# Softmax times V: eight adjacent rows in each partition, one row block as the unit of work, and the transposed probabilities as the stationary operand

## The chip, the cores and the metric

The kernel runs on one core of a Trainium2 chip. The metric is the device time of the whole program in microseconds, as the median of several timed runs. A separate, profiled execution gives the trace from which all durations are read.

## What is computed

```python
def setup_inputs():
    batch, n_heads, seq, head_dim = 8, 12, 1024, 64
    # scores: randn (8, 12, 1024, 1024) float32; v: randn (8, 12, 1024, 64) float32

def reference(scores, v):
    scores_max = np.max(scores, axis=-1, keepdims=True)
    attn = np.exp(scores - scores_max)
    attn = attn / (np.sum(attn, axis=-1, keepdims=True) + 1e-8)
    return np.matmul(attn, v).astype(np.float32)
```

There are 8 x 12 = 96 independent heads. Each one reads a score matrix of 1024 x 1024 fp32 numbers (4 MB) and a V of 1024 x 64 (256 KB), and writes 1024 x 64 (256 KB). Both kernels take the exponential without the row maximum, convert it to fp16, append a column of ones to V, so that the product also gives the row sums, and divide by them at the end.

## The kernel before

One pass of the loop over n works on one head. SyncE issues all DMAs. The load at L64 puts the head's scores into `s_nat` so that partition p holds rows p, 128 + p, 256 + p and so on: eight runs of 4 KB in each partition. V (L69) and the output (L151) are laid out in the same way, in runs of 256 bytes. `s_nat`, `p_nat` and most other tiles have two buffers.

ScalarE takes the exponential of the whole head in one instruction (L83, 8192 columns, into the fp16 tile `p_nat`) and converts V into `vones` (L91); VectorE writes its column of ones (L90). TensorE then needs the probabilities with the key index in the partitions. For each of the eight column blocks `jb` it transposes eight 128 x 128 blocks (L112) into a PSUM tile `psumT`, and VectorE copies the 1024 columns to SBUF as `pt` (L118). Two blocks later come the products (L101): `vones` of that block, 128 x 65, is the stationary operand, `pt` moves past it in two halves of 512 columns, and two PSUM tiles `psO` gather the 65 x 1024 result over the eight blocks. In a product or transpose the stationary operand is loaded first, by a LDWEIGHTS of its own (PEld in the profile).

The result then lies with the output column in the partitions. VectorE copies it to `outT` (L76), TensorE transposes it back in eight fp32 pieces (`psX`, L135), and VectorE takes the reciprocal of each piece's row sums (L143) and scales it (L144). The store at L151 follows. In the source the last steps of head n stand in the pass of head n + 1 (`prev`).

A scheduling layer fixes the order of each engine's instructions when the program is built; on each engine they then run in that order. In the steady state SyncE has the store of head n, then V of head n + 2 and the scores of head n + 3, one after the other. An instruction at the front of SyncE's order that waits holds up all behind it.

Of the kernel before, what the change touches and what calls it, by code (L numbers as in the profile page):

```python
# [1 line left out]

# [5 lines left out]

FP32 = mybir.dt.float32
FP16 = mybir.dt.float16  # L10


@with_exitstack
def kernel(
    ctx: ExitStack,
    tc: tile.TileContext,
    scores: bass.AP,
    v: bass.AP,
    out: bass.AP,
):  # L20
    nc = tc.nc
    P = 128

    B, H, SQ, SK = scores.shape
    Bv, Hv, SKv, D = v.shape
    assert (B, H, SK) == (Bv, Hv, SKv)
    BH = B * H
    assert SQ % P == 0 and SK % P == 0
    NIB = SQ // P
    NJB = SK // P  # L30
    CH = min(512, SQ)
    NCH = SQ // CH
    M = D + 1
    assert M <= P
    MMLAG = min(2, NJB)

    sc_bh = scores.rearrange("b h i j -> (b h) i j")
    v_bh = v.rearrange("b h j d -> (b h) j d")
    out_bh = out.rearrange("b h i d -> (b h) i d")

    const_pool = ctx.enter_context(tc.tile_pool(name="const", bufs=1))
    s_pool = ctx.enter_context(tc.tile_pool(name="spool", bufs=2))
    p_pool = ctx.enter_context(tc.tile_pool(name="ppool", bufs=2))
    v_pool = ctx.enter_context(tc.tile_pool(name="vpool", bufs=2))
    pt_pool = ctx.enter_context(tc.tile_pool(name="ptpool", bufs=4))
    ot_pool = ctx.enter_context(tc.tile_pool(name="otpool", bufs=2))
    ob_pool = ctx.enter_context(tc.tile_pool(name="obpool", bufs=2))
    rc_pool = ctx.enter_context(tc.tile_pool(name="rcpool", bufs=2))
    psT_pool = ctx.enter_context(tc.tile_pool(name="psTp", bufs=4, space=bass.MemoryType.PSUM))
    psO_pool = ctx.enter_context(tc.tile_pool(name="psOp", bufs=2, space=bass.MemoryType.PSUM))  # L50
    psX_pool = ctx.enter_context(tc.tile_pool(name="psXp", bufs=2, space=bass.MemoryType.PSUM))

    ident32 = const_pool.tile([P, P], FP32, name="ident32")
    make_identity(nc, ident32)
    ident16 = const_pool.tile([P, P], FP16, name="ident16")
    nc.vector.tensor_copy(out=ident16[:], in_=ident32[:])  # L56

    prev = None

    for n in range(BH + 1):  # L60
        cur = None
        if n < BH:
            s_nat = s_pool.tile([P, NIB, SK], FP32, tag="s_nat")
            nc.sync.dma_start(  # L64
                out=s_nat[:],
                in_=sc_bh[n].rearrange("(ib p) j -> p ib j", p=P),
            )
            v_sb = v_pool.tile([P, NJB, D], FP32, tag="v_sb")
            nc.sync.dma_start(  # L69
                out=v_sb[:],  # L70
                in_=v_bh[n].rearrange("(jb p) d -> p jb d", p=P),
            )

        if prev is not None:
            for c in range(NCH):
                nc.vector.tensor_copy(  # L76
                    out=prev["outT"][:, c * CH : (c + 1) * CH],
                    in_=prev["psO"][c][:],
                )

        if n < BH:
            p_nat = p_pool.tile([P, NIB, SK], FP16, tag="p_nat")
            nc.scalar.activation(  # L83
                out=p_nat[:],
                in_=s_nat[:],
                func=mybir.ActivationFunctionType.Exp,
            )

            vones = v_pool.tile([P, NJB, M], FP16, tag="vones")
            nc.vector.memset(vones[:, :, D : D + 1], 1.0)  # L90
            nc.scalar.copy(out=vones[:, :, 0:D], in_=v_sb[:])  # L91

            psO = [
                psO_pool.tile([M, CH], FP32, tag="psO", name=f"psO{c}")
                for c in range(NCH)
            ]
            pts = [None] * NJB

            def emit_mm(jb, psO=psO, pts=pts, vones=vones):
                for c in range(NCH):  # L100
                    nc.tensor.matmul(  # L101
                        out=psO[c][:],
                        lhsT=vones[:, jb, :],
                        rhs=pts[jb][:, c * CH : (c + 1) * CH],
                        start=(jb == 0),
                        stop=(jb == NJB - 1),
                    )

            for jb in range(NJB):
                psumT = psT_pool.tile([P, SQ], FP16, tag="psumT")  # L110
                for ib in range(NIB):
                    nc.tensor.transpose(  # L112
                        out=psumT[:, ib * P : (ib + 1) * P],
                        in_=p_nat[:, ib, jb * P : (jb + 1) * P],
                        identity=ident16[:],
                    )
                pt = pt_pool.tile([P, SQ], FP16, tag="pt")
                nc.vector.tensor_copy(out=pt[:], in_=psumT[:])  # L118
                pts[jb] = pt
                if jb - MMLAG >= 0:  # L120
                    emit_mm(jb - MMLAG)
            for jb in range(max(0, NJB - MMLAG), NJB):
                emit_mm(jb)

            outT = ot_pool.tile([M, SQ], FP32, tag="outT")
            cur = dict(n=n, psO=psO, outT=outT)

        if prev is not None:
            outT_p = prev["outT"]
            out_sb = ob_pool.tile([P, NIB, D], FP32, tag="out_sb")  # L130
            recip = rc_pool.tile([P, NIB], FP32, tag="recip")
            psXs = []
            for ib in range(NIB):
                psX = psX_pool.tile([P, M], FP32, tag="psX", name=f"psX{ib}")
                nc.tensor.transpose(  # L135
                    out=psX[:],
                    in_=outT_p[:, ib * P : (ib + 1) * P],
                    identity=ident32[0:M, 0:M],
                )
                psXs.append(psX)  # L140
            for ib in range(NIB):
                psX = psXs[ib]
                nc.vector.reciprocal(out=recip[:, ib : ib + 1], in_=psX[:, D : D + 1])  # L143
                nc.vector.tensor_scalar(  # L144
                    out=out_sb[:, ib, :],
                    in0=psX[:, 0:D],
                    scalar1=recip[:, ib : ib + 1],
                    scalar2=None,
                    op0=mybir.AluOpType.mult,
                )  # L150
            nc.sync.dma_start(  # L151
                out=out_bh[prev["n"]].rearrange("(ib p) d -> p ib d", p=P),
                in_=out_sb[:],
            )

        prev = cur


# [1 line left out]
_INS = ['scores', 'v']  # L160
_OUTS = [((8, 12, 1024, 64), 'float32')]


# [23 lines left out]
```

## Time and profile before

| | us |
|---|---|
| median of 3 timed runs (lowest to highest) | 1333.22 (1332.49 to 1334.44) |
| span of the profiled execution, first to last instruction | 1325.4 |
| TensorE busy with matmuls | 1049.5 |
| VectorE busy | 940.0 |
| ScalarE busy | 725.3 |

The span leaves out what lies ahead of the first and behind the last instruction; 7.8 us stand between it and the median. The busy times are sums over the span, and the engines work side by side, so no one of them is a share of the time by itself. The program moved 453.0 MB on SyncE's queue, which occupied sixteen DMA engines for 98.3% of the span.

### The profile page before, as it was taken

What the parts mean: (1) busy time and instruction counts of PE and PEld (TensorE: products, weight loads), DVE (VectorE), ACT (ScalarE), POOL (GpSimd) and SP (SyncE); (2) the same over time, 40 slices, a digit from 0 to 9 for tenths busy, and PEclk for the clock granted to TensorE, in tenths of its full rate; (3) what the DMA queues carried; (4) which work ended last, traced back from release to release, by engine and by line L of the source; (5) the groups of instructions that cost most, each with busy time, mean ns of one, the idle gap of its engine ahead of it and who ended that gap; (6) DMA issues with size and microseconds to landing.
All of it is one profiled execution on the core that took longest, in us unless ns stands there. A gap on an engine that the chain in (4) does not pass through costs nothing.

```text
span 1325.4 us, 21548 instructions
## 1 busy us (share of the span) xinstructions
PE 1049.5 (79%) x8448; PEld 739.9 (56%) x8448; DVE 940.0 (71%) x2593; ACT 725.3 (55%) x193; POOL 0.7 (0%) x6
## 2 busy tenths in 40 slices
PE   3888888787888887786887788888877878787776
PEld 2655565565655555554555455555655556554554
DVE  2777777767677777767777677767777767777676
ACT  4554655555464655555464555556465555646562
POOL 0000000000000000000000000000000000000000
PEclk9878777877778788888778878777788877988887
DMA  9999999999999999999999999999999999999993
GB/s 364 353 349 345 343 349 340 367 335 344 351 354 345 344 372 333 360 339 353 344 352 352 336 351 341 366 332 358 339 343 362 335 363 333 370 337 342 354 351 110
DMA packets 299620, 454.38 MB, mean 343 GB/s; under 512 B 201216, under 2 KB 201216, under 8 KB 299520
## 3 DMA queue, kind: packets, MB, share of 16 engines
q1 hardware_dynamic: 299520, 453.00, 98.3%
q8 instruction: 68, 1.11, 0.3%
q14 instruction: 32, 0.26, 0.0%
HBM read 427.82 MB, written 25.17 MB: 342 GB/s over the span
## 4 chain that ended last, share of the span: by engine, by line
PE 43%; DMA 26%; DVE 12%; ACT 12%; issue 4%; SPq 2%; ACTq 0%
DMA s_nat<-in_scores_dram 24%; PE psumT L112 22%; PE psO L101 17%; ACT p_nat L83 12%; DVE outT L76 5%; PE psX L135 4%; DVE out_sb L144 4%; DVE recip L143 3%; DMA v_sb<-in_v_dram 2%; SPq L69 1%; SPq L151 0%; ACT vones L91 0%; ACTq L83 0%; SPq L64 0%; ACTq L91 0%
## 5 line engine op out<-in xcount | busy, mean ns | idle before, releaser
L83 ACT ACTIVATE p_nat<-s_nat 128x8192 f16<-128x8192 f32 x96 | 675.0, 7031 | 582.6 <-DMA s_nat<-in_scores_dram 508.7
L118 DVE COPY pt<-psumT 128x1024 f16<-128x1024 f16 x768 | 526.4, 691 | 277.8 <-PE psumT L112 276.5
L112 PEld LDWEIGHTS <-p_nat 128*128 128x128 f16 x6144 | 506.1, 118 | 205.2 <-issue 68.0
L112 PE MATMUL psumT<-ident,p_nat 128*128 128x128 f16 x6144 | 562.5, 255 | 53.6 <-ACT p_nat L83 53.2
L101 PE MATMUL psO<-pt,vones 128*65 128x512 f16 x1536 | 493.1, 422 | 0.0
L135 PE MATMUL psX<-ident,outT 65*128 65x65 f32 x768 | 186.2, 270 | 218.3 <-DVE recip L143 72.4
L135 PEld LDWEIGHTS psX<-ident,outT 65*128 65x128 f32 x768 | 106.8, 149 | 328.3 <-PE psX L135 223.1
L144 DVE TENSOR_SCALAR out_sb<-psX,recip 128x64 f32<-128x64 f32 x768 | 209.2, 283 | 20.4
L101 PEld LDWEIGHTS <-vones 128*65 128x65 f16 x1536 | 157.5, 125 | 47.9 <-issue 17.9
L76 DVE COPY outT<-psO 65x512 f32<-65x512 f32 x192 | 123.4, 682 | 44.8 <-PE psO L101 44.8
L143 DVE RECIPROCAL recip<-psX 128x1 f32<-128x1 f32 x768 | 115.4, 160 | 37.8 <-PE psX L135 22.8
L91 ACT CAST vones<-v_sb 128x512 f16<-128x512 f32 x96 | 58.0, 604 | 0.0
L90 DVE MEMSET vones<- 128x8 f16 x96 | 6.2, 65 | 0.8 <-PEq L171 0.8
L83 ACT ACT_TABLE_LOAD x1 | 1.3, 1283 | 0.7 <-PEq L171 0.7
L56 DVE CAST ident<-ident 128x128 f16<-128x128 f32 x1 | 0.2, 227 | 0.4 <-POOL ident masks.py:199 0.4
masks.py:199 POOL TENSOR_SCALAR_AFFINE_SELECT ident<-ident 128x128 f32<-128x128 f32 x1 | 0.3, 292 | 0.1
masks.py:197 POOL MEMSET ident<- 128x128 f32 x1 | 0.2, 204 | 0.3 <-POOLq L171 0.3
L171 POOL MEMSET const-bfloat16-1.0<- 128x1 bf16 x1 | 0.1, 101 | 0.0
L171 POOL MEMSET const-uint8-127<- 128x1 uint8 x1 | 0.1, 101 | 0.0
L171 POOL MEMSET const-float32-0.0<- 128x1 f32 x1 | 0.1, 98 | 0.2 <-issue 0.2
L171 POOL MEMSET const-float32-1.0<- 128x1 f32 x1 | 0.1, 98 | 0.0
## 6 DMA issues: line engine op xcount, KB each, us to landing
s_nat<-in_scores_dram SPq DMA_DIRECT2D x96, 4096.0 KB, 17.7
v_sb<-in_v_dram SPq DMA_DIRECT2D x96, 256.0 KB, 7.2
out_dram<-out_sb SPq DMA_DIRECT2D x96, 256.0 KB, 6.6
```

The lines of the kernel that those rows point to most:

```text
L69: nc.sync.dma_start(out=v_sb[:], in_=v_bh[n].rearrange("(jb p) d -> p jb d", p=P),)
L76: nc.vector.tensor_copy(out=prev["outT"][:, c * CH : (c + 1) * CH], in_=prev["psO"][c][:],)
L83: nc.scalar.activation(out=p_nat[:], in_=s_nat[:], func=mybir.ActivationFunctionType.Exp,)
L90: nc.vector.memset(vones[:, :, D : D + 1], 1.0)
L91: nc.scalar.copy(out=vones[:, :, 0:D], in_=v_sb[:])
L101: nc.tensor.matmul(out=psO[c][:], lhsT=vones[:, jb, :], rhs=pts[jb][:, c * CH : (c + 1) * CH], start=(jb == 0), stop=(jb == NJB - 1),)
L112: nc.tensor.transpose(out=psumT[:, ib * P : (ib + 1) * P], in_=p_nat[:, ib, jb * P : (jb + 1) * P], identity=ident16[:],)
L118: nc.vector.tensor_copy(out=pt[:], in_=psumT[:])
L135: nc.tensor.transpose(out=psX[:], in_=outT_p[:, ib * P : (ib + 1) * P], identity=ident32[0:M, 0:M],)
L143: nc.vector.reciprocal(out=recip[:, ib : ib + 1], in_=psX[:, D : D + 1])
L144: nc.vector.tensor_scalar(out=out_sb[:, ib, :], in0=psX[:, 0:D], scalar1=recip[:, ib : ib + 1], scalar2=None, op0=mybir.AluOpType.mult,)
L171: nc = _bacc.Bacc("TRN2", target_bir_lowering=False, num_devices=1)
```

## The change

The layout of all three arrays changes: partition p now holds rows 8p to 8p + 7, so its share of the scores is one run of 32 KB, and its shares of V and of the output are runs of 2 KB. The unit of work is a row block r: row 8p + r of every partition p. The exponential is taken for two rows at a time (2048 columns). For the product the key index must be split as V's is: key 8q + c lies in partition q. So each transpose reads every eighth column of a row block (`p_row`), and eight of them make the tile `pt` of that row block. In the product `pt` is now the stationary operand (128 x 128) and `vones` the moving one (65 columns), and the result lands in PSUM with the rows in the partitions. There is no transpose back: for four row blocks at a time one reciprocal and one multiplication scale the result into `out_sb`. Products follow their transposes by two units.

V's conversion moves from ScalarE to GpSimd, into three permanent tiles whose ones are written once. There are more buffers: four for the scores, six for `p_nat`, five for `pt` and `psT`. The last head's scores come in four loads.

```diff
-    sc_bh = scores.rearrange("b h i j -> (b h) i j")
-    v_bh = v.rearrange("b h j d -> (b h) j d")
-    out_bh = out.rearrange("b h i d -> (b h) i d")
+    sc_bh = scores.rearrange("b h (p r) j -> (b h) p r j", p=P)
+    v_bh = v.rearrange("b h (p c) d -> (b h) p c d", p=P)
+    out_bh = out.rearrange("b h (p r) d -> (b h) p r d", p=P)
...
-    s_pool = ctx.enter_context(tc.tile_pool(name="spool", bufs=2))
-    p_pool = ctx.enter_context(tc.tile_pool(name="ppool", bufs=2))
-    v_pool = ctx.enter_context(tc.tile_pool(name="vpool", bufs=2))
-    pt_pool = ctx.enter_context(tc.tile_pool(name="ptpool", bufs=4))
...
+    s_pool = ctx.enter_context(tc.tile_pool(name="spool", bufs=4))
+    p_pool = ctx.enter_context(tc.tile_pool(name="ppool", bufs=6))
+    v_pool = ctx.enter_context(tc.tile_pool(name="vpool", bufs=4))
+    pt_pool = ctx.enter_context(tc.tile_pool(name="ptpool", bufs=5))
...
+    vones_bufs = []
+    for k in range(NV):
+        vo = const_pool.tile([P, C, M], FP16, name=f"vones{k}")
+        nc.vector.memset(vo[:, :, D : D + 1], 1.0)
+        vones_bufs.append(vo)
...
+    def finish(u):
...
+        n, r, pt, st = u
+        g = r % G
+        if g == 0:
+            st["psO"] = psO_pool.tile([P, G, M], FP32, tag="psO", name="psO")
+        psO = st["psO"]
+        for c in range(C):
+            nc.tensor.matmul(
+                out=psO[:, g, :],
+                lhsT=pt[:, c * P : (c + 1) * P],
+                rhs=st["vones"][:, c, :],
+                start=(c == 0),
+                stop=(c == C - 1),
             )
...
+        if g == G - 1:
...
+            nc.vector.reciprocal(out=recip[:], in_=psO[:, :, D : D + 1])
+            nc.vector.tensor_tensor(
+                out=st["out_sb"][:, r - G + 1 : r + 1, :],
+                in0=psO[:, :, 0:D],
+                in1=recip[:].to_broadcast([P, G, D]),
+                op=mybir.AluOpType.mult,
             )
+        if r == R - 1:
+            nc.sync.dma_start(out=out_bh[n], in_=st["out_sb"][:])
...
+    for n in range(BH):
+        last = n == BH - 1
+        v_sb = v_pool.tile([P, C, D], FP32, tag="v_sb", name="v_sb")
+        nc.sync.dma_start(out=v_sb[:], in_=v_bh[n])
+        s_nat = s_pool.tile([P, R, SK], FP32, tag="s_nat", name="s_nat")
+        step = EB if last else R
+        for r in range(0, R, step):
+            nc.sync.dma_start(out=s_nat[:, r : r + step, :], in_=sc_bh[n, :, r : r + step, :])
+
+        vones = vones_bufs[n % NV]
+        nc.gpsimd.tensor_copy(out=vones[:, :, 0:D], in_=v_sb[:])
+        st = dict(vones=vones)
+
+        for r in range(R):
+            if r % EB == 0:
+                p_nat = p_pool.tile([P, EB, SK], FP16, tag="p_nat", name="p_nat")
+                nc.scalar.activation(out=p_nat[:], in_=s_nat[:, r : r + EB, :], func=EXP)
+            p_row = p_nat[:, r % EB, :].rearrange("p (q c) -> p c q", c=C)
+            psT = psT_pool.tile([P, SK], FP16, tag="psT", name="psT")
+            for c in range(C):
+                nc.tensor.transpose(
+                    out=psT[:, c * P : (c + 1) * P],
+                    in_=p_row[:, c, :],
+                    identity=ident16[:],
                 )
...
+            pt = pt_pool.tile([P, SK], FP16, tag="pt", name="pt")
+            nc.vector.tensor_copy(out=pt[:], in_=psT[:])
+            pending.append((n, r, pt, st))
+            if len(pending) > LAG:
+                finish(pending.pop(0))
```

Two places show how the order moves. The first is SyncE at the start of the program. A number behind a name counts tiles; of the kernel before, `s_nat_517` belongs to head 3, `s_nat_670` to head 4 and `s_nat_823` to head 5, and the first three outputs are `out_sb_329`, `out_sb_482` and `out_sb_635`. Before:

```order
L64 DMA s_nat_517<-in_scores_dram 128x8x1024
L151 DMA out_0_dram<-out_sb_329 128x8x64
L151 DMA out_0_dram<-out_sb_482 128x8x64
L69 DMA v_sb_519<-in_v_dram 128x8x64
L64 DMA s_nat_670<-in_scores_dram 128x8x1024
L151 DMA out_0_dram<-out_sb_635 128x8x64
L69 DMA v_sb_672<-in_v_dram 128x8x64
L64 DMA s_nat_823<-in_scores_dram 128x8x1024
```

Now, with `s_nat_427` of head 2, `s_nat_602` of head 3 and `s_nat_777` of head 4, and with `out_sb_205`, `out_sb_380` and `out_sb_555` as the first three outputs:

```order
L104 DMA s_nat_427<-in_scores_dram 128x8192
L95 DMA out_0_dram<-out_sb_205 128x512
L95 DMA out_0_dram<-out_sb_380 128x512
L100 DMA v_sb_600<-in_v_dram 128x512
L104 DMA s_nat_602<-in_scores_dram 128x8192
L95 DMA out_0_dram<-out_sb_555 128x512
L100 DMA v_sb_775<-in_v_dram 128x512
L104 DMA s_nat_777<-in_scores_dram 128x8192
```

Before, the scores of heads 3 to 5 stood ahead of the first output and behind the second and third: three heads on. Now the scores of head 3 stand behind the store of head 1, and those of head 4 behind the store of head 2: two heads on.

The second place is VectorE at the end of the first head. The last copy of its `pt` comes first; before, the evacuation to `outT` and the pieces `psX` follow:

```order
L118 COPY pt_202<-psumT_193 128x1024
L76 COPY outT_210<-psO0_104 65x512
L76 COPY outT_210<-psO1_105 65x512
L143 RECIPROCAL recip_330<-psX0_331 128x1
L143 RECIPROCAL recip_330<-psX1_333 128x1
L90 MEMSET vones_372 128x8
L144 TENSOR_SCALAR out_sb_329<-psX0_331,recip_330 128x64
L144 TENSOR_SCALAR out_sb_329<-psX1_333,recip_330 128x64
L143 RECIPROCAL recip_330<-psX2_335 128x1
L144 TENSOR_SCALAR out_sb_329<-psX2_335,recip_330 128x64
```

Now, from the last three copies of the first head (`pt_195`, `pt_220`, `pt_240`) to the first of the second (`pt_266`):

```order
L123 COPY pt_195<-psT_186 128x1024
L87 RECIPROCAL recip_206<-psO_137 128x4
L123 COPY pt_220<-psT_211 128x1024
L88 TENSOR_TENSOR out_sb_205<-psO_137,recip_206 128x256
L123 COPY pt_240<-psT_231 128x1024
L87 RECIPROCAL recip_295<-psO_222 128x4
L88 TENSOR_TENSOR out_sb_205<-psO_222,recip_295 128x256
L123 COPY pt_266<-psT_257 128x1024
```

The evacuation, eight reciprocals and eight scalings of a head have become two reciprocals and two multiplications, and the second pair stands directly behind the head's last copy, ahead of the next head's first.

## Rows read from the trace of the kernel before

**Rows 1.** The page: engines; DMA packets; the queue that SP feeds (packets, MB, share).

```profile
PE 1049.5 (79%) x8448; PEld 739.9 (56%) x8448; DVE 940.0 (71%) x2593; ACT 725.3 (55%) x193; POOL 0.7 (0%) x6
...
DMA packets 299620, 454.38 MB, mean 343 GB/s; under 512 B 201216, under 2 KB 201216, under 8 KB 299520
...
q1 hardware_dynamic: 299520, 453.00, 98.3%
```

**Rows 2.** Waits, first of the engines, then of SyncE: total us, times, longest us.

```profile
ACT p_nat L83 <- DMA s_nat<-in_scores_dram: 508.7, 84, 11.9
...
SPq L151 <- DVE out_sb L144: 767.5, 96, 13.7
```

**Rows 3.** Stretches of the first load: us, PE busy, granted clock, DMA share, GB/s.

```profile
1.00:2.00 1.00, 0.00 (x0) 1.00 0.35 49
2.00:3.00 1.00, 0.00 (x0) 1.00 0.72 143
4.00:12.00 8.00, 0.00 (x0) 1.00 1.01 410
```

**Rows 4.** Stretches of a later head, same columns.

```profile
605.00:610.50 5.50, 3.87 (x30) 1.00 0.88 220
611.50:618.00 6.50, 3.31 (x27) 0.56 1.03 411
```

**Rows 5.** SyncE in order of time: start us, us, instruction.

```profile
0.73 0.43 SPq L64 DMA_DIRECT2D s_nat<-in_scores_dram  x1
1.23 0.57 SPq L69 DMA_DIRECT2D v_sb<-in_v_dram  x1
...
601.46 0.38 SPq L151 DMA_DIRECT2D out_dram<-out_sb  x1
```

**Rows 6.** The loads of L64 from issue to landing.

```profile
DMA to landing us min/median/max: 13.2/17.7/23.6
```

**Rows 7.** Groups by line: busy us, mean ns of one, idle before.

```profile
L83 ACT ACTIVATE p_nat<-s_nat 128x8192 f16<-128x8192 f32 x96 | 675.0, 7031 | 582.6 <-DMA s_nat<-in_scores_dram 508.7
L118 DVE COPY pt<-psumT 128x1024 f16<-128x1024 f16 x768 | 526.4, 691 | 277.8 <-PE psumT L112 276.5
...
L144 DVE TENSOR_SCALAR out_sb<-psX,recip 128x64 f32<-128x64 f32 x768 | 209.2, 283 | 20.4
...
L76 DVE COPY outT<-psO 65x512 f32<-65x512 f32 x192 | 123.4, 682 | 44.8 <-PE psO L101 44.8
L143 DVE RECIPROCAL recip<-psX 128x1 f32<-128x1 f32 x768 | 115.4, 160 | 37.8 <-PE psX L135 22.8
L91 ACT CAST vones<-v_sb 128x512 f16<-128x512 f32 x96 | 58.0, 604 | 0.0
...
masks.py:199 POOL TENSOR_SCALAR_AFFINE_SELECT ident<-ident 128x128 f32<-128x128 f32 x1 | 0.3, 292 | 0.1
```

**Rows 8.** TensorE in order of time, at both clock levels.

```profile
620.17 0.59 PE L101 MATMUL psO<-pt,vones 128*65 128x512 f16 x2
620.60 0.61 PE L112 MATMUL psumT<-ident,p_nat 128*128 128x128 f16 x8
621.04 0.59 PE L101 MATMUL psO<-pt,vones 128*65 128x512 f16 x2
...
630.04 1.06 PE L101 MATMUL psO<-pt,vones 128*65 128x512 f16 x2
630.89 1.06 PE L112 MATMUL psumT<-ident,p_nat 128*128 128x128 f16 x8
631.74 0.63 PE L101 MATMUL psO<-pt,vones 128*65 128x512 f16 x1
```

**Rows 9.** Stretches of 2 us: PE busy, granted clock, DMA share, GB/s.

```profile
608.00:610.00 2.00, 0.69 (x5) 1.00 0.80 158
...
612.00:614.00 2.00, 0.21 (x1) 0.57 1.03 406
...
618.00:620.00 2.00, 2.00 (x18) 0.72 0.98 298
```

More of the change, by code (lines that the diff above doesn't have):

```diff
@@ L10 @@
 FP16 = mybir.dt.float16
+EXP = mybir.ActivationFunctionType.Exp
 @with_exitstack
@@ L28 @@
     assert SQ % P == 0 and SK % P == 0
[L29 to L32, printed above, removed]
+    R = SQ // P
+    C = SK // P
     M = D + 1
-    assert M <= P
-    MMLAG = min(2, NJB)
-    sc_bh = scores.rearrange("b h i j -> (b h) i j")
-    v_bh = v.rearrange("b h j d -> (b h) j d")
-    out_bh = out.rearrange("b h i d -> (b h) i d")
-    const_pool = ctx.enter_context(tc.tile_pool(name="const", bufs=1))
-    s_pool = ctx.enter_context(tc.tile_pool(name="spool", bufs=2))
-    p_pool = ctx.enter_context(tc.tile_pool(name="ppool", bufs=2))
-    v_pool = ctx.enter_context(tc.tile_pool(name="vpool", bufs=2))
-    pt_pool = ctx.enter_context(tc.tile_pool(name="ptpool", bufs=4))
[L46 to L51, printed above, removed]
+    EB = 2
+    G = 4
+    LAG = 2
+    NV = 3
+    sc_bh = scores.rearrange("b h (p r) j -> (b h) p r j", p=P)
+    v_bh = v.rearrange("b h (p c) d -> (b h) p c d", p=P)
+    out_bh = out.rearrange("b h (p r) d -> (b h) p r d", p=P)
+    const_pool = ctx.enter_context(tc.tile_pool(name="const", bufs=1))
+    s_pool = ctx.enter_context(tc.tile_pool(name="spool", bufs=4))
+    p_pool = ctx.enter_context(tc.tile_pool(name="ppool", bufs=6))
+    v_pool = ctx.enter_context(tc.tile_pool(name="vpool", bufs=4))
+    pt_pool = ctx.enter_context(tc.tile_pool(name="ptpool", bufs=5))
+    ob_pool = ctx.enter_context(tc.tile_pool(name="obpool", bufs=3))
+    rc_pool = ctx.enter_context(tc.tile_pool(name="rcpool", bufs=4))
+    psT_pool = ctx.enter_context(tc.tile_pool(name="psTp", bufs=5, space=bass.MemoryType.PSUM))
+    psO_pool = ctx.enter_context(tc.tile_pool(name="psOp", bufs=3, space=bass.MemoryType.PSUM))
     ident32 = const_pool.tile([P, P], FP32, name="ident32")
@@ L56 @@
     nc.vector.tensor_copy(out=ident16[:], in_=ident32[:])
[L58 to L66, printed above, removed]
-            )
[L68 to L71, printed above, removed]
-            )
[L74 to L78, printed above, removed]
-                )
[L81 to L156, printed above, removed]
@@ new lines @@
+    vones_bufs = []
[3 more added lines that the diff above has]
+        vones_bufs.append(vo)
+    pending = []
+    def finish(u):
[11 more added lines that the diff above has]
+                stop=(c == C - 1),
+            )
+        if g == G - 1:
+            if r == G - 1:
+                st["out_sb"] = ob_pool.tile([P, R, D], FP32, tag="out_sb", name="out_sb")
+            recip = rc_pool.tile([P, G, 1], FP32, tag="recip", name="recip")
+            nc.vector.reciprocal(out=recip[:], in_=psO[:, :, D : D + 1])
[4 more added lines that the diff above has]
+                op=mybir.AluOpType.mult,
+            )
+        if r == R - 1:
+            nc.sync.dma_start(out=out_bh[n], in_=st["out_sb"][:])
@@ L160 @@
+    while pending:
+        finish(pending.pop(0))
 _INS = ['scores', 'v']
```

## The prediction

> **What bounds the kernel now.** I read the page first: no compute engine is full (TensorE 79% of the span, VectorE 71%, ScalarE 55%), while the queue that SyncE feeds fills 98.3% of sixteen DMA engines [rows 1]. The waits agree: ScalarE stands 508.7 us for score loads [rows 2]. So transfers bound it, but 453.0 MB in 1325.4 us is only 342 GB/s, and the stretches of one head say why. While score rows of 4 KB flow, the queue moves 411 GB/s; round the change from head to head it moves 220 GB/s at a DMA share of 0.88 [rows 4]. Two thirds of all packets are under 512 bytes [rows 1], the 256-byte runs of v and out. One head takes 1325.4/96 = 13.8 us; its 4.19 MB of scores at 411 GB/s take 10.2, so 3.6 us go to 0.52 MB of v and out and to holes. One more row matters: SyncE waits 767.5 us for the finished output before it may issue that store [rows 2], and each later load stands behind the store.
>
> **Transfers, part by part.** Bytes stay. v and out become 2 KB runs, scores 32 KB runs. For v and out the bounds are 0.52 MB at the 411 GB/s of 4 KB runs, 1.3 us, and today's 3.6; 2 KB lies by the first, so 1.3 us, and 11.5 us of DMA per head. Were 32 KB cut into 4 KB pieces again, the scores' 10.2 us would not move; for a gain there is no row, and I allow 5%, 0.5 us, as the lower end. If nothing else held the queue, a head would cost 11.5 us.
>
> **The order of issues.** Something else does. SyncE's order now has the store of head n, then v and scores of head n+2; before, the scores of n+3 followed it. Four score buffers exist, but only two heads are ahead. So the load of n+2 starts when head n is finished, and x, the time per head, obeys 2x = C + S, where C runs from the landing of a head's scores to its store's issue, and S from there to the landing two heads on.
>
> S: store and v take 0.38 and 0.57 us to issue, with gaps 1.1 us before the score load's own issue [rows 5]. A load's shortest issue-to-landing is 13.2 us [rows 6], so S is at most 14.3. That load crept in its first microseconds (49 and 143 GB/s, then 410) [rows 3]; first packets came about 1.1 us after issue, so without creeping S is 1.1 + 1.1 + 10.2 = 12.4. I take the middle, 13.35: the queue will have stood briefly, not since the start.
>
> C, engine by engine. **ScalarE:** one exp of 8192 columns (7.03 us) becomes four of 2048. From 7031 ns at 8192 and 604 at 512 columns [rows 7], 0.837 ns a column and 175 fixed, hence 1.89 us each, 7.6 a head; the cast of v leaves (0.60 us), so its sum stands still, but the first two rows are ready after 1.9 us, not 7. **GpSimd** takes that cast. The nearest row is 128 columns in 292 ns [rows 7]; the 512 columns cost between that, if it is all start cost, and four times it, 1.2 us. v lands before the scores, so I cost it at nothing; uncovered, 1.2 us in C would be 0.6 per head.
>
> **TensorE:** 64 transposes a head stay. At the full clock eight take 620.60 to 621.04, 0.44 us; at the half clock 0.85 [rows 8]. Sixteen products of 512 columns (0.43 us a pair) become 64 of 65 columns, and eight fp32 transposes go. No row has a 65-column pair of load and product. Lower bound: on the line through 128 and 512 columns, 29 ns at full clock, 53 at half; upper bound: the transposes' own 55 and 106, same 128-column load. I take the line, because load and stream overlap in the transposes already. A row unit (eight transposes, eight products) is then 0.67 us or 1.27. **VectorE:** eight copies of 0.69 stay; the evacuations, 768 scalings and 768 reciprocals become two reciprocals and two products of 256 columns a head, 0.45 each (between 283 ns at 64 and 682 at 512 columns [rows 7]). 6.7 us a head: never last.
>
> At full clock the exps pace: 7.6; then the last two rows' transposes and the products between (1.1), the last copy (0.7) and products (0.2), with gaps 2.4; then 1.0 for wait, reciprocal (0.16) and product (0.45) on VectorE: C = 11.0. At half clock TensorE paces: 1.9 + 8 x 1.27 + 1.0 = 13.1. Which clock? Today it was full through 608 to 610 though TensorE was busy 0.69 of 2 us, down to a mean of 0.57 in 612 to 614 after that thin stretch, and coming back in 618 to 620 under dense work [rows 9]. The new head leaves TensorE idle some 3 us and busy 9 to 11; neither level can be excluded, so the middle, C = 12.05.
>
> **The sum.** x = (12.05 + 13.35)/2 = 12.7. First landing: issue at 1.2, 13.2 after, 14.4; less 2.4, because the first three heads load back to back at 11.5; drain after the last landing 8.7 (its last quarter's exp 1.9, the rest of the chain 3.4, issue 0.4, store landing 3.0, an estimate); 7.8 lies outside the span (1333.2 - 1325.4). Time = 28.5 + 95x = 1235 us. With both unknowns at their ends x is 11.7 or 13.7: 1140 to 1330.
>
> **Two rules against the rows.** The new transposes load every eighth fp16 value, 16 bytes apart; no row here has such a load. The Trainium skill (SBUF — State Buffer, "Door 1: The DMA port swizzle") says SBUF has 16-byte lines and each access that crosses to a new line pays; no run here shows it, and its result is a rival below. Today's queue holds 411 GB/s over 6.5 us, one core running. The Trainium skill (DMA: Bandwidth & Descriptors, "Specifications") gives about 358 GB/s as the limit of HBM for each core; the trace disagrees. An estimate by that page: 453.0 MB would need 1265 us, and the time would be some 1290.
>
> **Rivals.** (a) *The queue never runs dry*: x = 11.5 gives 1121, down to 1045 at 10.7. It needs C under 9.7, and the exps with what follows them alone take 11.0; for it speaks only that S might be shorter. (b) *TensorE at half clock becomes the bound*, slower: if the small products cost as much as the transposes, 106 ns, a row unit is 1.70 us, C = 16.5, x = 14.9, 1444 us. It decides from 1.40 us a unit: then C passes 14.1 and x 13.73, the break-even. For it: today's second stretch at half clock stands amid dense work [rows 8]. Against: at half clock the new work is denser, and dense work raised the clock in 618 to 620 [rows 9]. (c) *Strided loads show*: if a transpose takes twice, a unit at half clock is 1.70 + 0.42 = 2.12, TensorE alone 17.0 a head, 1643 us. At full clock doubling gives 0.88 + 0.23 a unit, still near the exps' pace, so it too needs the half clock. (d) *Today's mean of 342 GB/s is a ceiling whatever the runs*: 1325.4 + 7.8 = 1333, no change; the 411 GB/s speak against it. (e) *The long runs do nothing*: cut into 4 KB, they leave the forecast where it is.
>
> **How the numbers follow.** Forecast 0.68 (0.02 of it within the measurement); (a) 0.08; (b) 0.13; (c) 0.09; (d) 0.02. About 0.2% (2.7 us) is what a measurement of this kernel can tell from no change. Faster 0.66 + 0.08 = 0.74, same 0.02 + 0.02 = 0.04, slower 0.13 + 0.09 = 0.22. The range takes in the forecast's ends, (a) at its first price, (b) to its price and (d): 1120 to 1445; it leaves out (c), the lower part of (a) and dearer cases of (b), together under 0.2. The forecast's own range is 1140 to 1330.
>
> **What would show it.** Right: the store still waits long for VectorE; score loads land 12.4 to 14.3 us after the store's issue; DMA has a hole at each head and its share is under 0.98; packets under 512 bytes are gone; eight transposes stay at 0.44 us, eight products near 0.23, at full clock; exp near 1.89. Wrong: DMA at 0.98 or more (a); TensorE without idle and at half clock (b); transposes above 55 ns at full clock (c). A load of n+2 that SyncE issues before head n's store would overturn the sum.

## The result and the profile after

The changed kernel takes 1281.15 us (median of 4 runs, 1278.68 to 1282.05) beside 1332.86 us for the kernel before on the same chip: 0.9615 of it, with a 95% interval of 0.960 to 0.963, or 52 us less. The forecast was 1235 us with a range of 1120 to 1445. The direction was right, and a little over half of the 98 us came. The profiled execution has a span of 1276.9 us.

The page of the changed kernel (engines; DMA packets; SyncE's queue with packets, MB and share; the chain that ended last):

```profile
PE 797.7 (62%) x12288; PEld 760.6 (60%) x12288; DVE 619.7 (49%) x1156; ACT 703.9 (55%) x385; POOL 60.1 (5%) x102
...
DMA packets 42023, 454.76 MB, mean 356 GB/s; under 512 B 4656, under 2 KB 4656, under 8 KB 29232
...
q1 hardware_dynamic: 41904, 453.00, 87.9%
...
DMA 51%; PE 23%; DVE 8%; ACT 8%; issue 6%; SPq 4%; ACTq 0%
```

Against [rows 1]: the packets fell from 299620 to 42023, and the short ones of V and out are gone (the 4656 left under 512 B are packets of 4 bytes, 16 for each of SyncE's 291 DMAs). The same 453.00 MB now fill 87.9% of the sixteen engines instead of 98.3%. Per head that is 0.879 x 1276.9 / 96 = 11.7 us instead of 13.6. By the packets in the two traces the scores went from 11.2 to 10.1 us a head, V and the output from 2.3 to 1.5. No engine is full and the transfers aren't either, so something makes the queue stand still. The waits say what (ScalarE; then SyncE; total us, times, longest us), and the last row is the time of a score load from issue to landing:

```profile
ACT p_nat L113 <- DMA s_nat<-in_scores_dram: 553.3, 92, 11.6
...
SPq L95 <- DVE out_sb L88: 1110.7, 96, 21.5
...
DMA to landing us min/median/max: 5.8/13.8/33.7
```

SyncE's wait for the finished output has grown from 767.5 to 1110.7 us [rows 2]. ScalarE's wait for scores, 508.7 before, is 553.3. One row of SyncE's order explains both. SyncE in order of time:

```profile
605.40 0.34 SPq L95 DMA_DIRECT2D out_dram<-out_sb  x1
605.84 0.38 SPq L100 DMA_DIRECT2D v_sb<-in_v_dram  x1
606.31 0.40 SPq L104 DMA_DIRECT2D s_nat<-in_scores_dram  x1
616.61 0.34 SPq L95 DMA_DIRECT2D out_dram<-out_sb  x1
617.04 1.07 SPq L100 DMA_DIRECT2D v_sb<-in_v_dram  x1
618.21 0.38 SPq L104 DMA_DIRECT2D s_nat<-in_scores_dram  x1
632.03 0.34 SPq L95 DMA_DIRECT2D out_dram<-out_sb  x1
```

and ScalarE over the same time (in brackets, how long it had stood and for what):

```profile
605.67 7.32 ACT L113 ACTIVATE p_nat<-s_nat 128x2048 f16<-128x2048 f32 x4 [4.43 <-DMA s_nat<-in_scores_dram]
...
620.08 7.32 ACT L113 ACTIVATE p_nat<-s_nat 128x2048 f16<-128x2048 f32 x4 [7.09 <-DMA s_nat<-in_scores_dram]
```

A head's scores land at 605.6 and its store is issued at 616.61: C = 11.0 us. The scores issued at 606.31, behind the store of 605.40, land at 620.0: S = 14.6 us. Behind its two loads SyncE does nothing until the next store is ready. Stretches of 1 us show the hole (us, PE busy, granted clock, DMA share, GB/s; a packet counts where it starts, so that a short stretch can pass 1):

```profile
603.00:604.00 1.00, 0.84 (x22) 1.00 1.21 524
604.00:605.00 1.00, 0.43 (x8) 1.00 0.06 16
605.00:606.00 1.00, 0.00 (x0) 1.00 0.00 0
...
617.00:618.00 1.00, 0.00 (x0) 0.72 0.50 201
618.00:619.00 1.00, 0.00 (x0) 0.50 0.71 250
```

Over heads 5 to 89 the trace gives a mean C of 11.59 us (11.04 to 12.25), a mean S of 14.85 us (13.33 to 16.97) and a mean of x = 13.23 us from landing to landing. That (11.59 + 14.85)/2 = 13.22 fits the prediction's 2x = C + S is no test: C and S together run from one landing to that two heads on, so their sum is 2x whatever the kernel does. The law says more, namely that the load starts with the store, and that what is added to C or S alone shows by half in x; the experiments try that. The heads by themselves take between 11 and 16 us, often a short one and a long one in turn.

The engines' own prices, by groups (busy us, mean ns of one, idle before), to be read with [rows 7]:

```profile
L113 ACT ACTIVATE p_nat<-s_nat 128x2048 f16<-128x2048 f32 x384 | 702.6, 1900 | 564.7 <-DMA s_nat<-in_scores_dram 553.3
L123 DVE COPY pt<-psT 128x1024 f16<-128x1024 f16 x768 | 529.1, 690 | 599.5 <-PE psT L117 587.3
...
L107 POOL CAST vones<-v_sb 128x512 f16<-128x512 f32 x96 | 59.4, 619 | 1196.0 <-DMA v_sb<-in_v_dram 1094.1
L88 DVE TENSOR_TENSOR out_sb<-psO,recip 128x256 f32<-128x256 f32 x192 | 80.6, 420 | 3.3
```

and TensorE's loads in order of time, at the full and at the half clock, to be read with [rows 8] (the start of one group to the start of the next is what it costs):

```profile
611.16 0.35 PEld L76 LDWEIGHTS <-pt 128*128 128x128 f16 x8
...
611.45 0.57 PEld L117 LDWEIGHTS <-p_nat 128*128 128x128 f16 x8
...
611.94 0.35 PEld L76 LDWEIGHTS <-pt 128*128 128x128 f16 x8
...
625.12 0.85 PEld L117 LDWEIGHTS <-p_nat 128*128 128x128 f16 x8
...
625.90 0.59 PEld L76 LDWEIGHTS <-pt 128*128 128x128 f16 x8
...
626.41 0.84 PEld L117 LDWEIGHTS <-p_nat 128*128 128x128 f16 x8
```

Eight small products take 0.29 us at full clock and 0.51 at half, eight transposes 0.49 and 0.78. The clock sets C, but not by its level at the landing. Both heads above begin their transposes at half clock, since it fell while TensorE stood idle (us, PE busy, granted clock, DMA share, GB/s):

```profile
607.20:610.61 3.41, 2.98 (x30) 0.50 1.01 369
610.62:616.61 5.99, 4.87 (x103) 1.00 1.01 438
617.44:627.67 10.23, 5.63 (x63) 0.50 0.94 375
```

In the head that landed at 605.6 it was back at 610.6, 5.0 us later, and C was 11.0; in the one that landed at 620.0 it was back at 627.7, 7.7 us later, and C was 12.0. Over heads 5 to 89 C goes with this one number: 11.04 to 11.07 us in the heads where the clock was back by 5.3 us, 11.5 at 6.3, 12.0 at 7.5 and 12.25 at 8.2. A likely reason is that the transposes of the first rows wait for the exponentials anyway, and those of the later rows do not.

### The profile page after: what moved, and what is told of

The parts are those of the page before. It is cut to its first block, busy times and chain, and to the rows that moved or that the text cites. A ratio compares the mean times of both kernels' runs of the same rounds, so it can differ in the third digit from the quotient of the medians.

```text
span 1276.9 us, 27588 instructions
## 1 busy us (share of the span) xinstructions
PE 797.7 (62%) x12288; PEld 760.6 (60%) x12288; DVE 619.7 (49%) x1156; ACT 703.9 (55%) x385; POOL 60.1 (5%) x102
## 2 busy tenths in 40 slices
DMA packets 42023, 454.76 MB, mean 356 GB/s; under 512 B 4656, under 2 KB 4656, under 8 KB 29232
## 3 DMA queue, kind: packets, MB, share of 16 engines
q1 hardware_dynamic: 41904, 453.00, 87.9%
## 4 chain that ended last, share of the span: by engine, by line
DMA 51%; PE 23%; DVE 8%; ACT 8%; issue 6%; SPq 4%; ACTq 0%
DMA s_nat<-in_scores_dram 51%; PE psT L117 17%; ACT p_nat L113 8%; PE psO L76 6%; DVE pt L123 4%; DVE out_sb L88 3%; SPq L100 2%; DVE recip L87 1%; SPq L95 1%; ACTq L113 0%; SPq L104 0%
## 5 line engine op out<-in xcount | busy, mean ns | idle before, releaser
L113 ACT ACTIVATE p_nat<-s_nat 128x2048 f16<-128x2048 f32 x384 | 702.6, 1900 | 564.7 <-DMA s_nat<-in_scores_dram 553.3
L117 PE MATMUL psT<-ident,p_nat 128*128 128x128 f16 x6144 | 634.9, 269 | 435.3 <-ACT p_nat L113 435.2
L123 DVE COPY pt<-psT 128x1024 f16<-128x1024 f16 x768 | 529.1, 690 | 599.5 <-PE psT L117 587.3
L117 PEld LDWEIGHTS <-p_nat 128*128 128x128 f16 x6144 | 538.5, 156 | 460.2 <-ACT p_nat L113 450.5
L76 PE MATMUL psO<-vones,pt 128*128 128x65 f16 x6144 | 345.6, 205 | 40.0 <-DVE pt L123 40.0
L76 PEld LDWEIGHTS <-pt 128*128 128x128 f16 x6144 | 298.4, 107 | 52.2 <-DVE pt L123 52.2
L107 POOL CAST vones<-v_sb 128x512 f16<-128x512 f32 x96 | 59.4, 619 | 1196.0 <-DMA v_sb<-in_v_dram 1094.1
L88 DVE TENSOR_TENSOR out_sb<-psO,recip 128x256 f32<-128x256 f32 x192 | 80.6, 420 | 3.3
L87 DVE RECIPROCAL recip<-psO 128x4 f32<-128x4 f32 x192 | 34.1, 178 | 50.0 <-PE psO L76 50.0
L63 DVE MEMSET vones<- 128x8 f16 x3 | 0.1, 65 | 0.8 <-PEq L143 0.8
```

Of the source, the lines that this page charges most:

```text
L63: nc.vector.memset(vo[:, :, D : D + 1], 1.0)
L76: nc.tensor.matmul(out=psO[:, g, :], lhsT=pt[:, c * P : (c + 1) * P], rhs=st["vones"][:, c, :], start=(c == 0), stop=(c == C - 1),)
L87: nc.vector.reciprocal(out=recip[:], in_=psO[:, :, D : D + 1])
L88: nc.vector.tensor_tensor(out=st["out_sb"][:, r - G + 1 : r + 1, :], in0=psO[:, :, 0:D], in1=recip[:].to_broadcast([P, G, D]), op=mybir.Al ...
L107: nc.gpsimd.tensor_copy(out=vones[:, :, 0:D], in_=v_sb[:])
L113: nc.scalar.activation(out=p_nat[:], in_=s_nat[:, r : r + EB, :], func=EXP)
```

## The experiments

Each ratio is to the kernel before on the same chip; its medians there lie between 1330.35 and 1332.86 us, so differences of 2 or 3 us between runs below say nothing.

**The store leaves SyncE's queue.** If the order (scores of head n+2 behind the store of head n) costs the time, taking the store to another queue must give it back.

```diff
-            nc.sync.dma_start(out=out_bh[n], in_=st["out_sb"][:])
+            nc.gpsimd.dma_start(out=out_bh[n], in_=st["out_sb"][:])
```

> The changed kernel with one word different: GpSimd issues the stores, so no load stands behind a store on SyncE. Theory (the loop 2x = C + S through SyncE's order sets the time; C 11.6, S 14.85, x 13.2 in the changed kernel): the loop is gone, four score buffers allow loads further ahead, the queue stays full and x falls to the packets' own time, 11.5 to 11.7 us a head; 1110 to 1150 us. Rival A (the transfers themselves are slow, for example because 32 KB packets arrive late or unevenly): the holes stay, 1250 us or more. Rival B (TensorE at half clock takes over): x 12.5 or more, over 1215 us, with TensorE without idle time.

Measured: 1094.71 us, 0.8221 of the kernel before (0.8208 to 0.8234), the fastest of all, and 15 us under the theory's range. Its page (packets; the queues of SyncE and of GpSimd) and SyncE's longest wait:

```profile
DMA packets 35879, 454.76 MB, mean 416 GB/s; under 512 B 4656, under 2 KB 4656, under 8 KB 23088
...
q1 hardware_dynamic: 28080, 427.83, 92.0%
q0 software_dynamic: 7680, 25.17, 5.7%
...
SPq L104 <- ACT p_nat L113: 680.8, 92, 7.4
```

SyncE no longer waits for an output; its longest wait lasts until ScalarE has freed one of the four score buffers. C is 11.85 us, no shorter than before, so the gain is not from a faster engine; a head takes 11.19 us, and the two queues fill 97.7%, 11.1 us a head, where the theory had counted on 11.5 to 11.7. Taking the store out of SyncE's order was worth 186 us, more than three times what the whole change gave. The edit does one thing besides: on GpSimd's queue the store travels in packets of 4 KB instead of 2 KB. That this is not what counts is seen below, where V goes to the same queue, with the same packets, and nothing is gained.

**Loads in quarters, the store left where it is.** The other way to break the law: the head's first rows come earlier and its last quarter has only two rows of work behind it, so C becomes short while the order stays.

```diff
-        step = EB if last else R
+        step = EB
```

> The changed kernel with each head's scores in four loads of two row blocks, SyncE's order of heads as it was. Theory (loop): the wait behind the store stays, but C, counted from the last quarter's landing, falls from 11.6 to some 6 us, because the exp of three quarters is done by then; (6 + 14.9)/2 = 10.4 is less than the transfers' 11.6, so the queue is full and the time 1110 to 1160 us. Rival A (C does not matter, transfers do): 1260 to 1300 us. Rival C (three more issues and semaphores a head lengthen S by 1.3 us or more and eat the gain): 1200 us or more.

Measured: 1112.39 us, 0.8354 (0.8343 to 0.8366), as the theory had it. SyncE's queue, and its wait for the output:

```profile
q1 hardware_dynamic: 82944, 453.02, 99.9%
...
SPq L95 <- DVE out_sb L88: 771.0, 96, 10.9
```

C, from the landing of the last quarter to the store's issue, is 5.6 us instead of 11.6. S grew to 17.35, since now the store and the loads behind it find the queue busy. The scores still stand behind the store, but at 2.9 us a quarter the queue has about two quarters of the next head left by then, and never runs dry. A long wait in front of a store is no loss by itself; it is one when nothing is left in flight.

**Both.** The two edits above together.

> The changed kernel with both cures at once: stores on GpSimd and scores in four loads a head. Theory (either one alone already fills the queue): nothing to add, the better of the two, 1085 to 1115 us. Rival (each leaves holes that the other closes): under 1080 us.

Measured: 1117.24 us, 0.8395 (0.838 to 0.8411): nothing added, 2 us over the theory's range, and 23 us more than with the store alone moved. Once the engines are full neither edit has anything left to give. A run of two rows is 8 KB instead of 32 KB, and the two queues fill 99.0%, 11.5 us of packets a head instead of 11.1. That the shorter runs make this difference is likely but not shown.

**A later store.** The law gives a price: what is added to C costs half per head. The last multiplication of each head is made three times (the same values are written again).

```diff
-            nc.vector.tensor_tensor(
-                out=st["out_sb"][:, r - G + 1 : r + 1, :],
-                in0=psO[:, :, 0:D],
-                in1=recip[:].to_broadcast([P, G, D]),
-                op=mybir.AluOpType.mult,
-            )
+            for _ in range(3 if r == R - 1 else 1):
+                nc.vector.tensor_tensor(
+                    out=st["out_sb"][:, r - G + 1 : r + 1, :],
+                    in0=psO[:, :, 0:D],
+                    in1=recip[:].to_broadcast([P, G, D]),
+                    op=mybir.AluOpType.mult,
+                )
```

> The changed kernel with the head's last multiplication made three times instead of once, so that the store is ready 2 x 0.42 = 0.84 us later; VectorE has idle time enough. Theory (loop): C grows by 0.84, x by half of that, 95 x 0.42 = 40 us: 1315 to 1327 us. Rival A (transfers alone): no change, 1277 to 1285 us. Rival D (one head after the other, x = C + something): the whole 0.84 shows, 1361 us.

Measured: 1319.86 us, 0.9908 (0.9893 to 0.9922), 38.7 us more than the change. C grew by 0.82 to 12.41, S stayed (14.90), and 95 x 0.82/2 = 39.0. Both rivals fell: transfers alone would have changed nothing, one head after the other would have given 1361. VectorE is busy for half of the span, yet 0.82 us of it counted, since it stood ahead of the store.

**Transposes of adjacent columns.** The strided reads leave: each transpose takes 128 adjacent columns of the row block, which the products then pair with other rows of V.

```diff
-            p_row = p_nat[:, r % EB, :].rearrange("p (q c) -> p c q", c=C)
+            p_row = p_nat[:, r % EB, :].rearrange("p (c q) -> p c q", c=C)
```

> The changed kernel with the transposes reading adjacent columns instead of every eighth, so that the products pair the probabilities with other rows of v; only the reading pattern is meant. Eight transposes took 0.49 us at full clock in the changed kernel and 0.44 in the kernel before. Theory (the stride costs 6 ns a transpose at full clock, nothing at half clock): transposes back at 0.44; about 0.2 us less in C, x less by 0.1 us, 1266 to 1278 us. Rival (the 0.49 has another cause): 0.49 stays and the time too, 1279 to 1284 us.

Measured: 1279.53 us, 0.9615 (0.9591 to 0.964); no difference from the change that these runs can tell (six of them, 1276.88 to 1288.75). The time lies in the rival's range, just outside the theory's; the transposes go with the theory. TensorE's loads at the full clock:

```profile
613.47 0.46 PEld L117 LDWEIGHTS <-p_nat 128*128 128x128 f16 x8
613.89 0.35 PEld L76 LDWEIGHTS <-pt 128*128 128x128 f16 x8
```

Eight transposes take 0.42 us instead of 0.49, so the stride does cost some 9 ns each at full clock. At half clock eight that follow products take 0.78 us with and without it, eight that follow an idle stretch 0.77 and 0.73. The Trainium skill (SBUF — State Buffer, "Door 1: The DMA port swizzle") says that an access which crosses to a new 16-byte line pays; the trace agrees in direction, with those 9 ns. C fell by 0.18 us as expected, but S rose by 0.17 to 15.02, and the gain was lost there. Why S rose is open.

**Scores in short runs again.** The scores alone go back to rows p, 128 + p, ..., so to runs of 4 KB. It asks what the 32 KB runs are worth, and whether S is long because one engine with a 32 KB packet comes in late.

```diff
-    sc_bh = scores.rearrange("b h (p r) j -> (b h) p r j", p=P)
+    sc_bh = scores.rearrange("b h (r p) j -> (b h) p r j", p=P)
```

> The changed kernel with the scores alone laid out as before, in 4 KB runs (partition p holds rows p, 128 + p, ...); out and v keep their 2 KB runs, so the output rows stand in another order, and that is the part of the computation that differs. S was 14.85 us in the changed kernel, over every bound of the prediction, and the last of the sixteen engines lands about 1.3 us after the middle one. Theory (a late engine is late by a whole 32 KB packet of 1.2 us; smaller packets share the delay): S falls by 0.7 to 1.2, but 4 KB packets take 0.5 us more a head; x less by 0.1 to 0.35, 1248 to 1275 us. Rival (the delay is the queue's start-up and has nothing to do with the packets' size): only the 0.5 us is left, half of it in x, 1298 to 1310 us.

Measured: 1320.17 us, 0.9922 (0.9903 to 0.994). The theory of the late engine fell: S rose to 15.68 us instead of falling, and the first and the last of the sixteen engines are as far apart as before (1.65 us on average, 1.68 in the change). The rival's range, up to 1310, was missed as well, since the packets cost more than its 0.5 us. Its queue:

```profile
q1 hardware_dynamic: 127536, 453.00, 90.8%
```

0.908 x 1318.4/96 = 12.5 us of packets a head instead of 11.7. S rose by 0.83 us, as much as the packets' time by 0.8, and 95 x 0.83/2 = 39 us is the difference from the change. So the 32 KB runs carry most of the change's 52 us, though 4 KB rows alone had shown 411 GB/s [rows 4]. Why packets of 32 KB take less time for the same bytes is not shown.

**V on ScalarE's queue.** What does S consist of? V's issue stands between store and scores.

```diff
-        nc.sync.dma_start(out=v_sb[:], in_=v_bh[n])
+        nc.scalar.dma_start(out=v_sb[:], in_=v_bh[n])
```

> The changed kernel with the 2 KB-run load of v (0.25 MB a head) issued by ScalarE instead of SyncE; on SyncE only the store of head n and then the scores of head n+2 are left. The law 2x = C + S had C = 11.59 us and S = 14.85 us in the profile of the changed kernel. Theory (the chain store issue -> scores landed sets the time, and what stands in it counts): the issue of v, 0.47 us between the store's issue and that of the scores, leaves S, so x falls by 0.24 us at the least, 95 x 0.24 = 23 us, about 1258 us; if v's packets (1.54 us of a head's 10.03 us of packets) also come mostly into the time in which the queue has no scores load, x falls by up to 0.55 us and the time is about 1229 us. Rival (S is set by what the sixteen engines have to move between two heads, whoever issues it): v's bytes only change their place, S stays 14.8 us, 1276 to 1284 us. Half-way point 1269 us.

Measured: 1276.51 us, 0.9583 (0.9556 to 0.9609), an interval that overlaps the change's. S fell by 0.45 us to 14.40, nearly the theory's 0.47, but C rose by 0.32 to 11.91: ScalarE's issue of V waits until GpSimd's cast has freed a buffer, and exponentials behind it waited too, 138.9 us in 29 waits:

```profile
ACT p_nat L113 <- POOL vones L107: 138.9, 29, 5.3
```

The edit had put a new wait into C, so it did not decide. (The 1.54 us that the expectation gives to V's packets are those of V and the output together; V's are half of it.)

**V on GpSimd's queue.** The same without that side effect.

```diff
-        nc.sync.dma_start(out=v_sb[:], in_=v_bh[n])
+        nc.gpsimd.dma_start(out=v_sb[:], in_=v_bh[n])
```

> The changed kernel with the load of v issued by GpSimd, which has nothing to do but the casts of v, so that nothing else waits behind it (when ScalarE issued it, S fell by 0.45 us to 14.40, but C rose by 0.32 us to 11.91, because ScalarE stood before some exponentials behind its own issue of v; 2x = 26.3 us). The store of head n and then the scores of head n+2 stay on SyncE. Theory (the chain store issue -> scores landed sets the time, whatever stands in it counts): C as in the changed kernel, 11.6 us, S 14.4 us, x = 13.0 us, 95 x 0.21 = 20 us less than the changed kernel's 1281, about 1261 us (1252 to 1268). Rival (the engines have the same bytes to move, so where v is issued does not matter, and the 4.6 us that its issue by ScalarE gave is all there is): 1274 to 1283 us. A second rival (it is not the store ahead of the scores but the number of DMAs in SyncE's queue that costs, so that taking either off gives what taking the store off gave): about 1095 to 1130 us.

Measured: 1282.67 us, 0.9638 (0.9618 to 0.9659): the theory of the issue fell, its rival held. SyncE and GpSimd in order of time:

```profile
605.37 0.33 SPq L95 DMA_DIRECT2D out_dram<-out_sb  x1
605.64 0.54 POOL L100 DMA_DIRECT2D v_sb<-in_v_dram  x1 [0.30 <-POOL vones L107]
605.79 0.38 SPq L104 DMA_DIRECT2D s_nat<-in_scores_dram  x1
```

The scores are issued 0.42 us after the store instead of 1.11 on average, and still S is 14.86 us (C 11.62). So the 0.7 us of issuing were not what S waits for. V itself has not left the interval: its issue waits for the cast, and that for the head's last products, so it still comes right behind the store. V now lands 11.9 us after its issue (median), against 3.1 in the change: its packets have moved in among those of the scores and use up what the earlier issue gave. It also rules out that the mere number of DMAs on SyncE mattered: taking V off gave nothing, taking the store off 186 us. That S did fall by 0.45 us with V on ScalarE, where V is issued with the store and lands in 3.2 us, isn't explained by these two runs. The later store left the load before less to finish behind it (0.3 us of its packets instead of 0.6), and 2x fell by only 0.1 us there.

**The kernel before with the new layouts.** Do the longer runs alone do what the change does? Only the three layouts and the columns that a transpose reads are changed.

```diff
-                in_=sc_bh[n].rearrange("(ib p) j -> p ib j", p=P),
+                in_=sc_bh[n].rearrange("(p ib) j -> p ib j", p=P),
...
-                in_=v_bh[n].rearrange("(jb p) d -> p jb d", p=P),
+                in_=v_bh[n].rearrange("(p jb) d -> p jb d", p=P),
...
-                        in_=p_nat[:, ib, jb * P : (jb + 1) * P],
+                        in_=p_nat[:, ib, :].rearrange("p (q c) -> p c q", c=NJB)[:, jb, :],
...
-                out=out_bh[prev["n"]].rearrange("(ib p) d -> p ib d", p=P),
+                out=out_bh[prev["n"]].rearrange("(p ib) d -> p ib d", p=P),
```

> The kernel before with the three layouts of the change alone (32 KB and 2 KB runs, transposes of every eighth column); tiles, order and engines as before, so SyncE keeps the scores of head n + 3 behind the store of head n. Theory (the layout takes some 2 us of transfers from each head, and the change gave most of it back through its order): transfers 11.6 us a head, TensorE's own row of work about 11.2 us at full clock, so x 11.6 to 12.5 and 1130 to 1220 us, faster than the changed kernel. Rival (the gain of the changed kernel comes from its new work unit, not from the runs): 1290 us or more.

Measured: 1286.06 us, 0.9661 (0.9642 to 0.9681), where the theory wanted 1130 to 1220 and the rival 1290 or more. The queue, the chain that ended last by engine, and TensorE's wait for probabilities:

```profile
q1 hardware_dynamic: 41472, 453.00, 87.5%
...
PE 73%; DVE 21%; issue 4%; DMA 1%; ACT 1%
...
PE psumT L112 <- ACT p_nat L83: 20.0, 1, 20.0
```

The transfers are relieved just as in the change, and the chain has gone over to TensorE and VectorE, 13.15 us a head, in which TensorE waits for probabilities only once, at the start: eight blocks of transposes and products, then the evacuation, eight transposes back and the scalings, one after the other.

**The kernel before with its store on GpSimd.** Does the order matter there as well?

```diff
-            nc.sync.dma_start(
+            nc.gpsimd.dma_start(
```

> The kernel before with its stores issued by GpSimd, nothing else. Theory (before, the packets themselves fill the queue, and the store's place in SyncE's order costs nothing): same time, 1315 to 1340 us. Rival (the wait behind the store cost the kernel before as well): 1290 us or less.

Measured: 1291.31 us, 0.9704 (0.9679 to 0.9729), faster than the theory had it, and 1 us over the rival's bound. ScalarE's longest wait is no longer for scores, TensorE waits for probabilities once, at the start, and SyncE waits for ScalarE:

```profile
ACT p_nat L83 <- PE psumT L112: 481.3, 86, 6.4
...
PE psumT L112 <- ACT p_nat L83: 21.1, 1, 21.1
...
SPq L64 <- ACT p_nat L83: 888.1, 84, 12.7
```

ScalarE stands until TensorE has read one of its two `p_nat` buffers: again the chain of TensorE, 13.05 us a head. Here too the edit does more than reorder: on GpSimd's queue the store's 256-byte packets become packets of 4 KB, half of all packets under 512 B are gone, and yet the two queues still show 98.2%. A full share of packets' time is thus no proof that transfers come last; whether TensorE waits is. So the kernel before had two limits within 5% of each other, transfers at 13.6 us a head and TensorE with VectorE at 13.05 to 13.15. Relieving the transfers, by layout or by queue, gives 3 to 3.4%.

## Why the prediction was half right

**What bounded the kernel.** Right that the transfers came last, but only by a little. The prediction did not see that the chain of TensorE and VectorE stood 0.4 to 0.6 us a head behind them, because idle sums (TensorE 21%, VectorE 29% of the span) were taken for slack. The trace of the kernel before had it, in the chain that ended last and in TensorE's wait for probabilities:

```profile
PE 43%; DMA 26%; DVE 12%; ACT 12%; issue 4%; SPq 2%; ACTq 0%
...
PE psumT L112 <- ACT p_nat L83: 53.2, 33, 21.0
```

The 53.2 us hold one wait of 21.0 for the first head, so late scores cost TensorE some 32 us of the whole run. The forecast was not hurt by this, since the new work unit shortens that chain as well; the two runs on the kernel before show it, and for them the expectations missed.

**Transfers.** 11.5 us of packets a head were forecast, 11.7 measured. What was wrong is where it came from: for the scores' long runs the forecast allowed nothing (0.5 us stood as a lower end), and the run with 4 KB rows shows 0.8 us a head for them; V and the output, taken at 1.3, are 1.5. Rival (e), that the long runs do nothing, fell, and so did (d), a ceiling at 342 GB/s. With the store moved the mean over the whole span was 416 GB/s, 414 of them by the bytes read from HBM and written to it. The Trainium skill (DMA: Bandwidth & Descriptors, "Specifications") gives about 358 GB/s as each core's limit; the measurement decides against it here.

**The order of issues.** Right, and it is the case's main result: the store waits, and the load of head n+2 stands behind it. The later store, with 0.82 us in C and the same S, gave the law's price to within 1 us, and the moved store took the law away. Both show it; the mean of C and S, as said, could not.

**C.** 12.05 us forecast, between 11.0 and 13.1; 11.59 measured. The prices of ScalarE, VectorE and GpSimd held, forecast against measured: exponential 1.89 and 1.90 us, multiplication 0.45 and 0.42, reciprocal 0.16 and 0.18, GpSimd's cast 0.3 to 1.2 and 0.62, the last one hidden. The small products were a fifth to a quarter too cheap: 29 ns against 36 (0.29 us for eight) at full clock and 53 against 64 at half. The clock question, left open between two levels, has neither level for an answer: the half clock lies in the first 8.2 us behind a landing and ends there, earlier in one head and later in another. Where it ends early C is the 11.0 forecast for the full clock; where it ends latest C is 12.25, and no head has the 13.1 of one that stays at half clock. In the head that landed at 620.0 eight transposes that start at 625.12 take 0.78 us, and eight that start at 628.46 take 0.49 again.

**S, the step that failed.** 13.35 us were taken, between 12.4 and 14.3; 14.85 were measured, above the upper end. Both ends left out the same thing. The lower one was 1.1 of issues, 1.1 to the first packet and 10.2 of scores; the upper one 1.1 and the shortest landing. But the store and V are issued just ahead of the scores, and their 0.52 MB, which the part on transfers had itself priced at 1.3 us a head, run in that same interval. With them the ends are 13.7 and 15.6, the middle 14.65, and 28.5 + 95 x (11.59 + 14.65)/2 = 1275 us. The run with V on GpSimd speaks for these bytes and against the issues: earlier scores, same S. It does not take the bytes away, though, and no run here does. What filled the interval can be counted in the trace. First the head above as a whole, then the mean of heads 5 to 89:

```profile
605.40:619.98 14.58, 7.86 (x128) 0.80 0.91 356
```

356 GB/s over 14.58 us are 5.2 MB, 1.0 more than the scores that were waited for. On average over the sixteen engines the 14.85 us hold 10.1 of the awaited scores' packets, 2.2 of the packets of stores and V's (also of the neighbouring heads'), 0.6 of the load before, which in 65 of 85 heads lands after the store's issue (2.3 us after it in these), and 1.8 without a packet. So the 10.2 for the scores and the 2.2 us without transfers (issues, first packet) of the lower end were about right; the packets of the two small DMAs and the rest of the load before were put at nothing and take 2.8. This says what S was filled with, not what S would lose if one of these went. The error of 1.50 us in S makes 71 us in time and that of 0.46 in C takes back 22, together the 49 us between 1235 and what 28.5 + 95 x 13.22 gives, 1284. That the two errors pull in opposite ways is luck, as is that the fixed 28.5 us came out some 3 too large: its 3.0 us for a store's landing had no row behind it, and the changed kernel's stores land after 2.4 us (median).

**Rivals.** (a), the queue that never runs dry, is what moving the store makes true: 1095 us where (a) had 1121. (b) and (c) fell: TensorE has idle stretches between heads, a row unit takes 0.78 us at full and 1.29 at half clock, under the 1.40 from which (b) decides, and strided loads cost some 9 ns, not twice the time.

**The signs named beforehand.** Holes at each head, a DMA share under 0.98, no packets under 512 bytes of V or out, and the long wait of the store came as said. Score loads land 14.85 us after the store's issue instead of 12.4 to 14.3, eight small products take 0.29 us at full clock instead of 0.23, and eight transposes 0.49 instead of 0.44. That is 61 ns for one transpose, over the 55 named as the sign of (c); its direction was right, and its size is too small to matter here.

## What to carry to other kernels

A queue that is served in order ties a load to whatever stands ahead of it: look for a store that waits for the end of the computation with the next loads behind it, and give it a queue of its own. The time of such a loop is (landing to store + store to landing) divided by the number of heads ahead. That sum is always true; it becomes a forecast only when both parts are forecast, and into the second go all bytes that are released at the same moment, not only the ones waited for. Before a full resource is relieved, ask which chain comes next: here it stood 3 to 4% behind. Relieving the transfers alone gave 3%, and relieving both, with the store out of the loads' way, 18%.

## What the hardware showed that was not expected

Runs of 32 KB are worth something over 4 KB in the time of packets, 11.7 against 12.5 us a head for the same bytes, 6%. One core kept 416 GB/s over 1093 us. Strided reads of every eighth fp16 value cost a transpose some 9 ns at the full clock, and at half clock 5 ns behind an idle stretch and none behind products. And a half clock in the first 5 us of a head cost nothing, in each further us some 0.4 us.
